# The second layer's modulation, computed beside the first layer's gates and pools instead of beside its dense expert units

## The chip, the cores and the metric

One NeuronCore of a Trainium2 chip; the kernel uses one core. The metric is the device time of one execution in microseconds (us). The engines are named as the profile names them: PE (TensorE, matmuls) and PEld (its weight loads), DVE (VectorE), ACT (ScalarE), POOL (GpSimd) and SP (SyncE, which here issues DMAs only).

## The reference

Two blocks run one after the other on 256 tokens of width 1024, in fp32; the change is within the first. It has two layers, each of a mixer (differential attention, a pool branch and a convolution branch, merged by three sigmoid gates) and of a product-key expert layer. Each layer begins with its modulation:

```python
for l in range(DEPTH):
    mod = (jax.nn.silu(c) @ w_mod[l] + b_mod[l]).reshape(b, N_MOD, 1, d)
    mod_c = (jax.nn.silu(c_ctx) @ w_mod[l] + b_mod[l]).reshape(N_MOD, 1, 1, d)
    ...
    xn = modulate(rms_norm(h, norm1_g[l]), mod[:, 0], mod[:, 1])
    ...
    h = h + mod[:, 2] * mix
    xn2 = modulate(rms_norm(h, norm2_g[l]), mod[:, 3], mod[:, 4])
    h = h + mod[:, 5] * peer_ffn(xn2, ...)
```

`c` and `c_ctx` are inputs, so the modulation of both layers depends on nothing that the layers compute. `w_mod[l]` is 1024 x 6144 in fp32, 25.2 MB a layer.

## The kernel before, in words

**A modulation step.** `modulation(l, pairs)` (line 610) computes two of the six vectors of layer l for each member of `pairs`. For one pair it goes through eight steps, one for each 128 rows of `w_mod`: it loads 1 MB (128 partitions of 2048 numbers) into a raw tile and makes four matmuls with 32 columns of stationary operand each, one in each quarter of the output's partitions (line 626; the trace holds two records for each, eight a step). It yields after each step. After the eighth, the sum is copied by ScalarE (`modsb`), turned by four small matmuls (`ps_modt`, line 634), and VectorE adds the bias into `self.mod`.

A step's raw tile comes from one of three places: a list given to it (the first layer's pair 0, at the kernel's start), a pool given to it (tile `mraw`, lines 619 to 621), or `self.raw` (line 623), which the weight loads use too. In the mixer `self.raw` hands out the two `wraw` tiles by turns. In the first layer's dense expert stage it hands out three by turns: every third comes from the pool of the V units (`vraw`).

**Weights.** `wload` (line 348) loads 1 MB into such a raw tile, and ScalarE and VectorE split it into two units, each of a high part (`uhi`, `vhi`, line 361) and a low part (`ulo`, `vlo`, line 362). There are four units of the `u` kind. A raw tile is free again once both units are split, and a unit can be split once the matmuls on the one that had its place are done. All raw loads are issued by SyncE, whose queue is worked through in order; so are the other engines' queues. The order of each queue is laid down when the program is built, near the order in which the code issues, with instructions moved ahead of others that the builder expects to be ready later.

**The mixer's gate and pool stage.** The first layer works on 512 columns (256 tokens and 256 of context). Its work is paired by hand: `spread` (line 953) runs attention steps, and after each of them as many steps of a second generator, `feed`, as a rate allows (0.75 a step here). In the last part of the attention that second generator is `gate_pool`: eight pieces of weights, 16 products of 24 matmuls of 512 columns each (a pool or a gate), and the pool arithmetic on VectorE and POOL. `weaver` (line 173) puts modulation steps between the products. Of `n` steps it takes one, and then products until their number reaches the share (i + 1) * MODS / n, with MODS = 17. Modulation steps count nothing in the rate, so they come on top. Before, the steps are the 16 of pairs 1 and 2 of the first layer, all through the one tile `mraw`. What is left of the generator when attention ends is run in `mixer_out` (line 1020), ahead of the output product.

**The dense expert stage.** `peer` (line 1092) multiplies through all 16384 experts of the layer in 64 units of 256. In the first layer 384 of the 512 columns go this way, and the other 128 are handled by gathering single rows of u and v (class `Rows`; POOL issues a gather of 128 rows at a time, and VectorE multiplies the rows of u, while TensorE sums those of v in `ps_row`). 42 of the 64 units had their hidden values computed earlier, during routing, and stored in DRAM; the other 22 compute them here. The units go in turns of two and two until the 22 are used up (44 units), and then 20 with stored values follow. One unit loads a V piece (1 MB), the gates G (768 KB), and either a U piece (1 MB) or the stored values (384 KB). Its matmuls: 36 on V (`keep` and `ps_v`, line 1269) and, where hidden values are computed, 48 more (`ps_mm`). For two of the six 512-column products of a unit VectorE adds the result to `racc` (line 1236). The gathers are paced by the TensorE work done, not by time (`Rows.spend`). Before, one modulation step of the second layer is taken at each second unit from the third on (units 2, 4, ... 48), 24 steps in all, with raw tiles of the ring of three.

Of the kernel before, what the change touches and what calls it, by code (L numbers as in the profile page):

```python
# [37 lines left out]
MODS = 17  # L38
# [134 lines left out]
def weaver(main, n, fill, m):  # L173

    done = 0.0
    fill = iter(fill)
    for i, _ in enumerate(islice(main, n)):
        yield 0
        while done * n < (i + 1) * m:
            size = next(fill, None)  # L180
            if size is None:
                break
            done += size
            yield size
    yield from fill
# [144 lines left out]
class Prog:  # L330
# [279 lines left out]
    def modulation(self, l, pairs, raws=None, pool=None, bufs=3):  # L610

        nc, g = self.nc, self.g
        for m2 in pairs:
            ps = self.pm.tile([P, 512], F32, tag="mm", name="ps_mod")
            for k in range(KD):
                src = g["wmod"][l, m2 * KD + k]
                if raws:
                    raw = raws.pop(0)
                elif pool:
                    raw = pool.tile([P, 2048], F32, tag="mraw", name="mraw", bufs=bufs)  # L620
                    nc.sync.dma_start(raw, src)
                else:
                    raw = self.raw("wraw_m")
                    nc.sync.dma_start(raw, src)
                for c in range(4):
                    nc.tensor.matmul(ps[32 * c:32 * c + 32, :], self.sc[:, k, :], raw[:, c * 512:(c + 1) * 512],
                                     start=(k == 0), stop=(k == KD - 1), tile_position=(0, 32 * c))
                if k < KD - 1:
                    yield 0.18
            sb = self.sp.tile([P, 512], F32, tag="t2k", name="modsb")  # L630
            nc.scalar.activation(sb, ps, AF.Copy)
            pp = self.pm.tile([P, 4, 2, 2, 2], F32, tag="mm", name="ps_modt")
            for j in range(4):
                nc.tensor.matmul(pp[:, j].rearrange("p m i s -> p (m i s)"), sb[:, j * P:(j + 1) * P],
                                 self.sel.rearrange("p c s -> p (c s)"), start=True, stop=True)
            for m in (2 * m2, 2 * m2 + 1):
                mod = self.mod[:, l, m]
                b = self.col["bmod", l][:, m * 8:(m + 1) * 8]
                nc.vector.tensor_tensor(mod.rearrange("p (i j) s -> p i j s", i=2), pp[:, :, m % 2].rearrange("p j i s -> p i j s"),
                                        b.rearrange("p (i j) -> p i j", i=2)[:, :, :, None].to_broadcast([P, 2, 4, 2]), op=ALU.add)  # L640
                if m in (1, 4):
                    gn = self.col["n1" if m == 1 else "n2", l]
                    nc.vector.tensor_scalar(mod, mod, 1.0, None, op0=ALU.add)
                    nc.vector.tensor_tensor(mod, mod, gn[:, :, None].to_broadcast([P, KD, 2]), op=ALU.mult)
            yield 0.3
# [261 lines left out]
    def mixer(self, l, xh, xl, T, late, hT):  # L907
        nc, g, tc = self.nc, self.g, self.tc
        qts = list(range(T // P))
        merged = self.mp.tile([P, KD, T], F32, tag="merged", name="merged")  # L910
        self.merged, self.begun, self.pooled = merged, set(), set()
        outer = self.mp
        qkvs, self.done, self.scored, self.whole = {}, set(), set(), set()
        with ExitStack() as right:
            with ExitStack() as cx:
                E = cx.enter_context
                self.mp = E(tc.tile_pool(name=f"att{l}", bufs=1, reuse_waits="tile"))
                self.pa = E(tc.tile_pool(name=f"pa{l}", bufs=2, space=PSUM, reuse_waits="tile"))
                self.pt = E(tc.tile_pool(name=f"pt{l}", bufs=2, space=PSUM, reuse_waits="tile"))
                self.po = E(tc.tile_pool(name=f"po{l}", bufs=1, space=PSUM, reuse_waits="tile"))  # L920
                with tc.tile_pool(name=f"conv{l}", bufs=1, side="right", reuse_waits="tile") as mp:
                    yh = mp.tile([P, KD, T], F32R, tag="yh", name="yh")
                    yl = mp.tile([P, KD, T], F32R, tag="yl", name="yl")
                    conv = self.conv(l, xh, xl, yh, yl, mp, T)
                    next(conv)
                    if late:
                        late()
                    self.ropes(l, self.mp)
                    bulk = Bulk(chain(conv, self.conv_out(l, xh, xl, yh, yl, T)))
                    for _ in self.qkv(l, 0, xh, xl, T, qkvs, islice(bulk, MIX[l][0])):  # L930
                        pass
                    att = Bulk(self.attention(l, qkvs, qts, xh, xl, T))
                    feed = self.feed(l, xh, xl, T, qkvs, bulk)
                    self.steps = 0
                    self.spread(att, feed, MIX[l][2], bulk)
                mp = right.enter_context(tc.tile_pool(name=f"pool{l}", bufs=1, side="right", reuse_waits="tile"))
                mods = self.modulation(0, [1, 2], pool=mp, bufs=1) if l == 0 else iter(())
                bulk.steps, bulk.over = weaver(mods, 16, self.gate_pool(l, xh, xl, mp, T), MODS), False
                self.spread(att, feed, MIX[l][3], att)
            self.mp = outer  # L940
            return self.mixer_out(l, merged, hT, T, right, bulk)
# [150 lines left out]
    def peer(self, l, hT, T, xh, xl):  # L1092
        nc, g, tc = self.nc, self.g, self.tc
        T0, T = T, T - (NROW if l == 0 else 0)
# [5 lines left out]
        with ExitStack() as cx:  # L1100
# [23 lines left out]
            with ExitStack() as c:  # L1124
# [18 lines left out]
                late = []  # L1143
                self.gcur = None
                cur = self.prep(l, jobs[0], xh, xl, T, gd, hd)
                mods = self.modulation(1, range(3)) if l == 0 else iter(())
                for n in range(64):
                    if n % 2 == 0 and n > 1:
                        next(mods, None)
                    nxt = self.prep(l, jobs[n + 1], xh, xl, T, gd, hd) if n < 63 else None  # L1150
                    cur += (self.wload(g[f"v{l}"][jobs[n]], "v"),)
                    if n >= 64 - NLAST and onto:
                        late.append(cur)
                    elif n < 63 or onto:
                        self.values(l, cur, hT, T, keep, rest_acc, n == 0, not onto and n == 62)
                    if n < 1 and onto:
                        self.store_gates(GPARTS)
                    if n < 63:
                        cur = nxt
# [12 lines left out]
                else:  # L1172
                    self.preload("wb0", (1, 3))
                    row = self.rowof(lambda c_: self.mod[:, l, 5, c_, 0:1])
                    xh, xl = (self.xp.tile([P, KD, 512], F32R, tag=nm, name=nm) for nm in ("xh", "xl"))
# [753 lines left out]
```

## Time and profile before

| | |
|---|---|
| time, median of 3 runs | 3701.9 us (3687.57 to 3704.51) |
| the profiled execution's own time | 3701.45 us |
| its span, first to last instruction | 3699.7 us |
| mean granted TensorE clock | 0.985 of full speed |
| TensorE busy | 3574.0 us, 97% of the span |
| VectorE, ScalarE, POOL busy | 67%, 44%, 16% |
| DMA | 777.60 MB, mean 210 GB/s |
| modulation loads in the gate stage | 16 of 1 MB (`mraw`) |
| modulation loads in the dense stage | 24 of 1 MB (`wraw_m`) |

The page divides the span into 40 slices of 92.5 us and gives each engine's busy share in tenths. A window gives for one stretch the busy time of each engine with its number of records, the granted clock, the mean busy share of the 16 DMA engines and what they moved. A wait names the engine and line that waited, what ended the wait, the sum in us, how often, and the longest. In a timeline each row is an instruction with its start and duration, and in brackets the idle time of its engine before it and what ended that. Matmuls are pipelined and their ends are modelled, so records overlap, and a busy TensorE isn't one at its peak.

The first layer's mixer ends at about 700 us of the span, with the gate and pool stage from 490 to 642. Routing follows, and the dense expert stage from 1229 to 2105.

### The profile page before, as it was taken

To read this page: it belongs to the slowest core of one execution; us is meant where nothing else is said; L and a number is where in the kernel's file an instruction comes from. 1 tells how busy PE (TensorE), PEld (TensorE's weight loads), DVE (VectorE), ACT (ScalarE), POOL (GpSimd) and SP (SyncE) were. 2 spreads that over 40 slices of the span, in tenths; PEclk is the share of its full clock that TensorE was granted. 3 is DMA by queue.
4 is the path that set the end of the run, shared out by engine and by line. 5 is a ranking of instruction groups with operands and counts; after the bars stand their busy time and mean duration, and the time that the engine had idled before them with its cause. 6 is when DMAs were issued, how large, how long until landed. Compare 5 with 4: busy or idle time off the path is not lost.

```text
span 3699.7 us, 55016 instructions
## 1 busy us (share of the span) xinstructions
PE 3574.0 (97%) x21681; PEld 3097.0 (84%) x21681; DVE 2461.5 (67%) x4540; ACT 1634.3 (44%) x2608; POOL 604.0 (16%) x686
## 2 busy tenths in 40 slices
PE   7999999899999998999999999999999999999999
PEld 5988877789999877776766799999998888887787
DVE  5566556599697777744445677778876555557675
ACT  3334333336576322222222354555676444445454
POOL 0112222100011232322222121221000000002121
PEclk9999999999999999999999999999999999999999
DMA  5222145224689898888889533354578766766453
GB/s 212 75 86 80 69 154 216 75 83 170 228 323 336 315 332 306 325 295 309 298 321 325 188 115 120 120 175 160 200 269 292 244 236 237 242 231 212 145 174 111
DMA packets 227763, 777.60 MB, mean 210 GB/s; under 512 B 17296, under 2 KB 100752, under 8 KB 168496
## 3 DMA queue, kind: packets, MB, share of 16 engines
q1 hardware_dynamic: 165984, 567.29, 43.7%
q0 software_dynamic: 37184, 135.41, 10.4%
q10 hardware_dynamic: 24336, 71.38, 5.0%
q8 instruction: 170, 2.79, 0.3%
q14 instruction: 89, 0.73, 0.1%
HBM read 705.60 MB, written 68.42 MB: 209 GB/s over the span
## 4 chain that ended last, share of the span: by engine, by line
PE 41%; DVE 4%; DMA 2%; ACT 1%; issue 1%; POOL 1%; DVEq 0%; ACTq 0%; SPq 0%; POOLq 0%
PE keep L1269 12%; PE ps_mm L393 5%; PE ps_mm L395 5%; PE ps_mm L394 5%; PE ps_wide L395 2%; PE ps_wide L393 2%; PE ps_wide L394 2%; PE ps_v L1269 1%; DVE ulo L362 1%; PE ps_nar L393 1%; PE ps_nar L395 1%; PE ps_nar L394 1%; DMA wraw<-in_v 1%; PE ps_mm L414 1%; PE ps_row L307 1%
## 5 line engine op out<-in xcount | busy, mean ns | idle before, releaser
L361 ACT ACTIVATE uhi<-wraw 128x1024 fp32r<-128x1024 f32 x586 | 609.0, 1057 | 879.2 <-PE ps_mm L394 336.1
L393 PE MATMUL ps_mm<-xh,uhi 128*128 128x256 f32 (+2 forms) x2952 | 955.5, 324 | 9.2 <-ACT hs L1566 3.7
L395 PE MATMUL ps_mm<-xh,ulo 128*128 128x256 f32 (+2 forms) x2952 | 940.8, 319 | 7.1 <-DVE ulo L362 7.1
L362 DVE TENSOR_TENSOR ulo<-wraw,uhi 128x1024 fp32r<-128x1024 f32 x586 | 718.0, 1237 | 340.6 <-ACT uhi L361 317.6
L394 PE MATMUL ps_mm<-xl,uhi 128*128 128x256 f32 (+2 forms) x2952 | 939.9, 318 | 0.0
L393 PEld LDWEIGHTS ps_mm<-xh,uhi 128*128 128x128 f32 x2952 | 562.5, 191 | 54.0 <-issue 9.2
L395 PEld LDWEIGHTS ps_mm<-xh,ulo 128*128 128x128 f32 x2952 | 562.2, 191 | 29.4 <-DVE ulo L362 8.0
L394 PEld LDWEIGHTS ps_mm<-xl,uhi 128*128 128x128 f32 x2952 | 562.7, 191 | 20.8
L362 DVE TENSOR_TENSOR vlo<-wraw,vhi 128x1024 fp32r<-128x1024 f32 x184 | 224.0, 1222 | 187.7 <-ACT vhi L361 187.5
L361 ACT ACTIVATE vhi<-wraw 128x1024 fp32r<-128x1024 f32 x184 | 193.2, 1056 | 338.1 <-DMA wraw<-in_v 176.0
L1269 PE MATMUL keep<-vlo,Wh 128*128 128x512 f32 x656 | 256.7, 391 | 3.6 <-DVE vlo L362 3.6
L1269 PE MATMUL keep<-vhi,Wh 128*128 128x512 f32 x656 | 257.8, 393 | 0.5 <-ACT Wh L422 0.5
L1269 PE MATMUL keep<-vhi,Wl 128*128 128x512 f32 x656 | 256.2, 391 | 0.3 <-DVE Wl L423 0.3
L258 POOL DMA_INDIRECT row<-in_urow,eu x128 | 158.5, 1238 | 589.7 <-PE ps_mm L395 440.7
L1213 DVE TENSOR_TENSOR hs_r<-hs_r,G 128x768 f32<-128x768 f32 (+1 forms) x128 | 105.2, 823 | 170.7 <-DMA hs_r<-hd 106.9
L393 PE MATMUL ps_nar<-uhi,xh 128*128 128x256 f32 x704 | 201.3, 286 | 2.3 <-ACT cs L664 2.3
L394 PE MATMUL ps_nar<-ulo,xh 128*128 128x256 f32 x704 | 200.1, 284 | 0.0
L395 PE MATMUL ps_nar<-uhi,xl 128*128 128x256 f32 x704 | 199.9, 284 | 0.0
L258 POOL DMA_INDIRECT row<-in_vrow,ev x128 | 136.0, 1063 | 375.4 <-PE keep L1269 180.2
L1530 ACT ACTIVATE stage<-ps_g 128x512 f32<-128x512 f32 x160 | 165.1, 1160 | 1.7 <-DMA wraw<-in_u 0.8
L274 DVE CUSTOM_DVE_ANT_0 row<-row,xt 128x1024 f32<-128x1024 f32 x128 | 155.2, 1219 | 4.5 <-DMA row<-in_urow,eu 4.5
L1269 PEld LDWEIGHTS keep<-vhi,Wh 128*128 128x128 f32 x656 | 123.7, 189 | 36.8 <-issue 9.2
(428 smaller groups left out, 6965.2 us busy)
## 6 DMA issues: line engine op xcount, KB each, us to landing
wraw<-in_u SPq DMA_DIRECT2D x128, 1024.0 KB
wraw<-in_v SPq DMA_DIRECT2D x128, 1024.0 KB
wraw<-in_wa SPq DMA_DIRECT2D x104, 1024.0 KB
wraw<-in_wb SPq DMA_DIRECT2D x50, 1024.0 KB
gd<-stage ACTq DMA_DIRECT2D x80, 512.0 KB
wraw_m<-in_wmod SPq DMA_DIRECT2D x24, 1024.0 KB
G<-gd SPq DMA_DIRECT2D x31, 768.0 KB
mraw<-in_wmod SPq DMA_DIRECT2D x16, 1024.0 KB
```

The lines of the kernel that those rows point to most:

```text
L258: ins = self.nc.gpsimd.indirect_dma_start(row, None, self.p.g[name], bass.IndirectOffsetOnAxis(ap=idx, axis=0))
L274: ins = nc.vector.tensor_tensor_reduce(out=row, in0=row, in1=self.xt, op0=ALU.mult, op1=ALU.add, scale=1.0, scalar=0.0, accum_out=self.hid ...
L307: nc.tensor.matmul(ps[c:c + 32, :], m[:, g, :], rows[n - 4 + g][:, h * 512:(h + 1) * 512], start=(i == 0), stop=(i == 31), tile_position=( ...
L361: nc.scalar.activation(hi, r, AF.Copy)
L362: nc.vector.tensor_tensor(lo, r, hi.bitcast(F32), op=ALU.subtract)
L393: nc.tensor.matmul(ps, lh, rh, start=(i == 0), stop=False)
L394: nc.tensor.matmul(ps, lh, rl, start=False, stop=False)
L395: self.beat = nc.tensor.matmul(ps, ll, rh, start=False, stop=(i == n - 1))
L414: self.nc.tensor.matmul(ps[:, t0:t1], a[:, s], b[:, k, t0:t1], start=(n == 0 and i == 0), stop=(n == KD - 1 and i == 2))
L1213: nc.vector.tensor_tensor(w, w, G.rearrange("p q j t -> p j q t"), op=ALU.mult)
L1269: self.beat = self.nc.tensor.matmul(ps, a[:, j, t], b[:, c], start=(start and j == 0 and i == 0), stop=(stop and j == 1 and i == 2), skip_ ...
L1530: nc.scalar.activation(st[:, :, tb:tb + 4].rearrange("p j t -> p t j"), pg, AF.Copy, scale=1.0 / GSCALE)
```

## The change

The 24 steps of the second layer's modulation are chained behind the 16 of the first in the weaver of the gate and pool stage, which now spreads 40 steps over its 16 products. The tile `mraw` stays single, and each odd step takes its raw tile from `self.raw` instead, that is, one of the two `wraw` tiles. The dense stage's loop takes no modulation steps any more. By the weaver's sums a product now comes after two or three steps where it came after each step, and the last four steps come after the last product.

```diff
                 if raws:
                     raw = raws.pop(0)
-                elif pool:
+                elif pool and (bufs > 1 or k % 2 == 0):
                     raw = pool.tile([P, 2048], F32, tag="mraw", name="mraw", bufs=bufs)
                     nc.sync.dma_start(raw, src)
                 else:
...
-                mods = self.modulation(0, [1, 2], pool=mp, bufs=1) if l == 0 else iter(())
-                bulk.steps, bulk.over = weaver(mods, 16, self.gate_pool(l, xh, xl, mp, T), MODS), False
+
+                mods = chain(self.modulation(0, [1, 2], pool=mp, bufs=1), self.modulation(1, range(3), pool=mp, bufs=1)) if l == 0 else iter(())
+                bulk.steps, bulk.over = weaver(mods, 40, self.gate_pool(l, xh, xl, mp, T), MODS), False
                 self.spread(att, feed, MIX[l][3], att)
...
                 cur = self.prep(l, jobs[0], xh, xl, T, gd, hd)
-                mods = self.modulation(1, range(3)) if l == 0 else iter(())
                 for n in range(64):
-                    if n % 2 == 0 and n > 1:
-                        next(mods, None)
                     nxt = self.prep(l, jobs[n + 1], xh, xl, T, gd, hd) if n < 63 else None
```

## Rows read from the trace of the kernel before

**Rows 1.** The page's slices (92.5 us): busy tenths, TensorE and DMA engines.

```profile
PE   7999999899999998999999999999999999999999
DMA  5222145224689898888889533354578766766453
```

**Rows 2.** Windows: us; busy us (records) of each engine, PEclk, DMA share, GB/s.

```profile
core 0: us, PE busy (x) PEld busy (x) DVE busy (x) ACT busy (x) POOL busy (x), PEclk, DMA share, GB/s
490.00:642.00 152.00, 151.55 (x774) 112.89 (x773) 88.41 (x156) 55.19 (x121) 34.91 (x55) 1.00 0.54 195
1229.00:1600.00 371.00, 343.60 (x1617) 286.46 (x1617) 270.20 (x371) 107.62 (x130) 119.41 (x96) 0.96 0.87 313
1600.00:1900.00 300.00, 296.84 (x1517) 210.94 (x1516) 133.45 (x183) 79.23 (x94) 82.81 (x79) 1.00 0.87 307
1900.00:1955.00 55.00, 48.98 (x227) 31.67 (x226) 26.74 (x37) 14.18 (x16) 13.21 (x12) 0.95 0.92 347
1955.00:2045.00 90.00, 90.00 (x416) 62.02 (x416) 48.93 (x68) 22.15 (x25) 25.52 (x24) 0.98 0.90 315
```

**Rows 3.** Dense stage in windows of 20 us, columns of rows 2.

```profile
1320.00:1340.00 20.00, 16.09 (x73) 13.33 (x67) 15.57 (x20) 5.02 (x6) 4.39 (x5) 0.91 0.93 362
1340.00:1360.00 20.00, 20.00 (x106) 17.30 (x105) 13.85 (x20) 5.81 (x8) 6.78 (x6) 1.00 0.83 296
...
1380.00:1400.00 20.00, 14.63 (x65) 12.55 (x65) 13.23 (x20) 4.53 (x6) 4.63 (x5) 0.90 0.77 283
```

**Rows 4.** Waits to 1600 us (us, times, longest), TensorE and ScalarE.

```profile
PE ps_mm L393 <- DVE racc L1236: 16.1, 6, 4.5
...
ACT uhi L361 <- DMA wraw<-in_v: 97.1, 12, 14.2
```

**Rows 5.** Timeline of VectorE at one hole (start us, us, instruction, idle).

```profile
1329.22 2.36 DVE L362 TENSOR_TENSOR ulo<-wraw,uhi 128x1024 fp32r<-128x1024 f32 x2 [2.71 <-ACT uhi L361]
...
1332.64 0.68 DVE L1236 TENSOR_TENSOR racc<-racc,ps_v 128x512 f32<-128x512 f32 x1
```

**Rows 6.** SyncE's waits, 1600 to 1955 us.

```profile
SPq L351 <- PE ps_mod L626: 42.4, 9, 9.7
```

**Rows 7.** Timeline of TensorE, one modulation step, dense stage.

```profile
1319.52 0.40 PE L1269 MATMUL ps_v<-uhi,Wl 128*128 128x512 f32 x1
1319.85 1.06 PE L626 MATMUL ps_mod<-wraw_m,sc 128*32 128x512 f32 x8
1320.84 0.50 PE L1269 MATMUL keep<-uhi,Wh 128*128 128x512 f32 x1
1321.18 0.39 PE L1269 MATMUL keep<-ulo,Wh 128*128 128x512 f32 x1
```

**Rows 8.** Window of the kernel's start, columns of rows 2.

```profile
15.00:20.00 5.00, 3.98 (x11) 2.30 (x12) 1.03 (x3) 0.00 (x0) 1.03 (x1) 1.00 1.01 421
```

**Rows 9.** Timelines of SyncE, then ScalarE, in the gate stage.

```profile
529.89 0.33 SPq L621 DMA_DIRECT2D mraw<-in_wmod  x1
530.27 0.42 SPq L975 DMA_DIRECT2D pwr<-in_wa  x1
...
560.55 8.14 SPq L621 DMA_DIRECT2D mraw<-in_wmod  x2
...
570.22 0.43 SPq L975 DMA_DIRECT2D pwr<-in_wa  x1
...
535.36 0.63 ACT L422 ACTIVATE pwh<-pwr 128x512 fp32r<-128x512 f32 x1 [6.84 <-DMA pwr<-in_wa]
...
577.58 0.63 ACT L422 ACTIVATE pwh<-pwr 128x512 fp32r<-128x512 f32 x1 [6.71 <-DMA pwr<-in_wa]
```

**Rows 10.** Gate stage: ps_mod's window, idle before mraw's matmuls, SyncE's wait.

```profile
490.00:642.00 152.00, 17.05 (x128) 2.52 (x128) 1.04 (x2) 1.00 0.54 195
...
  issue: 2.7, 11
...
SPq L621 <- PE ps_mod L626: 59.6, 15, 9.1
```

## The prediction

> **What bounds the kernel now.** I began with the page's slices [rows 1]: TensorE is at 9 tenths nearly throughout, so the question is what its busy time hides in the two stages that the change touches. The slices show where they differ: in slices 12 to 22, which hold the dense stage, the DMA engines are at 8 or 9 tenths, in the mixer before it (slices 2 to 8) at 1 to 5. The change carries 24 loads of 1 MB out of the first stretch into the second.
>
> Then the stages by themselves [rows 2]. The gate and pool stage (490 to 642 us) has TensorE busy 151.55 of 152 us at full clock, with 195 GB/s: bound by TensorE, with no hole in it. The dense stage runs from 1229 to 2105 us, and falls into three. To 1600 us, while rows of u are gathered, TensorE is idle for 27.4 of 371 us and its granted clock is 0.96; DMA is at 313 GB/s. From 1600 to 1900 it is idle for 3.2 of 300 us. From 1900 to 1955 it is idle for 6.0 of 55 us at clock 0.95, at 347 GB/s. After 1955, when the last modulation load is done, it is not idle at all (90.00 of 90). The work is of one kind from 1900 us on (units with no hidden products), so its records tell the pace: without the 24 of modulation 203 in 55 us before 1955, 3.7 a us, and 416 in 90 us after it, 4.6 a us.
>
> [...] What ends a hole is mostly the sum into racc on VectorE, 16.1 us in six waits, and that stands in VectorE's queue behind the split of a weight unit that waited, by way of ScalarE, for a V load: 97.1 us of ScalarE's waits are for wraw<-in_v [rows 4]. Around 1329 us VectorE is seen to stand 2.71 us before ulo, and racc comes only after it [rows 5]. So V loads land late. They are late because SyncE issues them late: a raw tile must first be free, and a modulation raw is free only when TensorE has reached its matmuls; SyncE waited 42.4 us for that from 1600 on [rows 6].
>
> [...]
>
> **The change, part by part.**
>
> *Matmuls of a modulation step.* One step is 8 records in 1.06 us (24 steps: three pairs of eight in the code); from its start to the next matmul are 0.99 us, and the matmuls on its two sides stand 0.10 and 0.11 us further apart than the usual 0.23 [rows 7]. That is 1.2 us a step, 24 x 1.2 = 28.8 us that leave the dense stage, where TensorE sets the pace but for the holes. They come into the gate stage, which has 0.45 us idle to take them in: with two or three steps in a row some edges are shared, so 24 x 0.99 = 24 at least, 28.8 at most; I take 26. The three transpositions with their copies and additions move too, as much out of the one stage as into the other: nothing in the sum.
>
> *Loads out of the dense stage.* 25.2 MB leave a stretch of 726 us. What they are worth beyond the matmuls: to 1600 us, the holes (27.4 us) and the slow clock after them. Window by window the clock's loss is 4% of 371 = 15 us, of which some 6 lie within the holes. I take 60% of 27.4 + 9 = 36, that is 22: two of the ring's eight loads in four units are modulation, but the row gathers that stay load VectorE and the DMA queues as before. From 1600 to 1900: 2 of 3.2. From 1900 to 1955: 203 records at the later pace of 4.6 a us are 44 us, so 11 us, of which three steps are 3.6; of the other 7.5 I take 5. With 28.8 the dense stage gives 28.8 + 22 + 2 + 5 = 58 us. Bounds: 28.8 if no wait goes; 28.8 + 36 + 3 + 8 = 76 if all go. SyncE's order, the ring's turn (every third raw comes from the v pool) and the row pacing, which counts TensorE's work and not time, stay as they are but for the missing places.
>
> *Loads into the gate stage.* There, 16 steps went with 16 products, all through the single tile mraw; now 40 do, by turns through mraw and the two wraw tiles, which the weights of the same stage use. The page's 195 GB/s x 152 us = 29.6 MB become 54.8 MB in about 178 us, 308 GB/s; the start of the kernel moves 421 with the same 8 KB rows [rows 8], so bandwidth isn't short. Time from issue to landing is: the last of three loads (a mraw, a wraw, a quarter MB) issued from 568.4 to 570.2 us is awaited until 577.6, 9.2 us; with one mraw ahead, issued at 529.9, the quarter MB is there at 535.4, 5.5 us [rows 9]. Without its steps a product and its share of attention takes (152 - 17.05) / 16 = 8.4 us. Two steps come with 0.8 product: 6.7 + 2.0 = 8.7 us of cover for two loads and 0.4 weight load. It is near even. Where three steps stand in a row and the first uses mraw, the third waits for a load begun after the first: 5.5 - 1 = 4.5 us open. By the weaver's sums that is at steps 12 to 14, 26 to 28 and, with no product left, 36 to 39: 13 us. Before, none was: TensorE lost 2.7 us at all 16 steps [rows 10], with 9.5 us of cover each, though SyncE waited 59.6 us for ps_mod. Bounds: nothing, as the queues' order is laid out anew when the program is built and other products may stand in between; and 20 pairs x (9.2 - 8.7 + 2.4 for the splits) = 57 us if each pair ends on its loads (2.36 us for two on VectorE [rows 5], ScalarE's taken as long). I take 13, nearest to the rows of before, where the queue held.
>
> *Behind the loads.* On SyncE the weights of the last gates, the four loads of old and the first of w_out stand behind the last four steps. TensorE then has the six merged splits to wait for anyhow; within the 13. The first layer's modulation is complete earlier, the second's long before its use behind the dense stage: nothing. POOL's queue has none of these DMAs.
>
> **Sum.** -58 + 26 + 13 = -19 us. The profiled execution is 3701.45 us (span 3699.7 and 1.75 around it), the median of the three runs 3701.9, so the two agree: 3701.9 - 19 = **3683**.
>
> **Rivals.** *A, the gate stage becomes bound by its raw tiles.* Its pairs end on loads, not on TensorE: 26 + 57, against 58: +25, 3727; with only 28.8 from the dense stage +54, 3756. It decides the sign from 32 us of stalls on (58 - 26), 1.6 us a pair. For it: cover and load time are near even, SyncE is in order and already waits 59.6 us for ps_mod. Against: not one product waited before, and split weights lie up to four units ahead. [...]
>
> *B, the dense stage's holes have another cause.* VectorE is busy 270 of 371 us to 1600 [rows 2], much of it with row products that stay; if they are what delays the splits, only 28.8 us come back, and the gate stage takes 26 to 31: 3699 to 3704. For it: holes nearly vanish after 1600 us (3.2 of 300 us) though modulation goes on, when VectorE's busy time falls to 133 of 300. Against: after the last modulation load none is left.
>
> *C, the dense stage was bound by DMA.* 25.2 MB at 313 GB/s are 80 us; TensorE's own work holds that to 76. With 13 + 26 in the gate stage, 3665; with no stalls there, 3652. For it: 347 GB/s where the units take 55 us. Against: from 1600 to 1900 TensorE is full at 307 GB/s.
>
> **How the numbers follow.** A measurement of this kernel can tell about 0.5%, 18.5 us, from no change. The forecast (0.42) lies across that bound, -8 to -32; I put 0.25 of it on faster. C has 0.20, all faster. B has 0.19, all same. A has 0.19, 0.17 of it slower by over 18.5 us. Slower by over that for reasons of the rebuilt order takes 0.04 more from the forecast. So faster 0.45, same 0.34, slower 0.21. The range reaches to C's 3652 and over most of A, to 3724; the likeliest case by itself is 3670 to 3694.
>
> **What would show it.** Right: ps_mod in the gate stage with 320 records, that stage 30 to 50 us longer; from 1229's counterpart on no ps_mod, the 60 us period at 53 to 56 us, clock above 0.97, the dense stage 50 to 65 us shorter. Wrong by A: TensorE idle before ps_mod or before the gates' ps_mm, by a DMA of mraw, wraw_m or wraw, over 32 us in all. Wrong by B: holes of 4 us still there with no modulation near them.

## The result and the profile after

The changed kernel takes 3650.85 us (median of 4 runs, 3646.74 to 3653.45), the kernel before 3699.03 (median of 4, 3687.57 to 3704.51). The ratio is 0.9871 with a 95% interval of 0.9852 to 0.9889: 48 us faster. The forecast was 3683, 19 us faster, in a range from 3652 to 3724. The direction was right, the gain more than twice the forecast, and the time 1.2 us below the range.

Where did it go? I cut both executions at the same events. The first is `old`, the residual that is added behind the mixer's output product; the next is the first `keep` matmul, with which the dense stage begins. The slices answer [rows 1]: what they had at 8 and 9 tenths of DMA in the dense stage is still there, and the mixer's slices 6 to 8 have gone from 4, 5 and 2 tenths to 5, 7 and 6.

Page of the kernel after, busy tenths of TensorE and the DMA engines in slices of 91.2 us:

```profile
PE   7999999989999999999999999999999999999999
DMA  5222257623479999988799433354677766666343
```

The addition of `old` in the trace of the kernel before (first and last start, in us, stand after the durations):

```profile
L1088 DVE SCALAR_TENSOR_TENSOR hT<-ps_mm,mod,old x16: 473/475/484, 660.7 to 697.6; 128x256 f32<-128x256 f32 x16
```

The same in the kernel after, and under it the matmuls of modulation:

```profile
L1089 DVE SCALAR_TENSOR_TENSOR hT<-ps_mm,mod,old x16: 474/477/484, 701.7 to 738.6; 128x256 f32<-128x256 f32 x16
...
L626 PE MATMUL ps_mod<-mraw,sc x160: 592/592/617, 497.1 to 679.9; 128*32 128x512 f32 x160
L626 PE MATMUL ps_mod<-wraw_m,sc x160: 592/592/617, 504.3 to 680.8; 128*32 128x512 f32 x160
```

So all 320 matmuls lie in the gate and pool stage, half of them through `mraw`, half through the two `wraw` tiles, and the mixer ends 41.0 us later (660.7 to 701.7).

The dense stage I divide where the rows of `u` are done and the first rows of v are summed (first `ps_row`). *Part 1* is from the first `keep` to there, *part 2* from there to the last matmul that reads `racc`. Windows of the kernel before, with the columns of rows 2:

```profile
1243.20:1598.20 355.00, 327.60 (x1524) 271.32 (x1522) 258.47 (x355) 101.07 (x122) 112.90 (x90) 0.96 0.86 313
1598.20:2109.60 511.40, 502.21 (x2492) 352.61 (x2492) 245.91 (x348) 136.39 (x160) 132.90 (x127) 0.99 0.84 300
```

Windows of the kernel after, the gate and pool stage first:

```profile
490.00:702.00 212.00, 202.47 (x1073) 138.71 (x1072) 98.58 (x182) 63.23 (x133) 40.80 (x55) 0.98 0.71 267
1283.90:1580.80 296.90, 296.90 (x1420) 258.86 (x1418) 257.57 (x351) 100.82 (x121) 112.98 (x90) 1.00 0.94 334
1580.80:2060.70 479.90, 479.90 (x2382) 347.58 (x2381) 243.83 (x342) 135.49 (x158) 141.86 (x127) 1.00 0.84 292
```

| us | before | after | difference |
|---|---|---|---|
| start to the first `old` | 660.7 | 701.7 | +41.0 |
| first `old` to the first `keep` (routing) | 582.5 | 582.2 | -0.3 |
| dense, part 1 | 355.0 | 296.9 | -58.1 |
| dense, part 2 | 511.4 | 479.9 | -31.5 |
| last `racc` to the end | 1590.1 | 1589.2 | -0.9 |
| span | 3699.7 | 3649.9 | -49.8 |

In the dense stage TensorE now has no idle time at all, and the granted clock is 1.00. The 58.1 us of part 1 are three things. 27.4 us are idle time that is gone (355.0 - 327.60). 14.4 are, by the estimate of 1.2 us a step, the matmuls of 12 steps. The other 16.3 of the busy time (327.60 - 296.90 - 14.4) are for the most part work that TensorE did slowly behind holes: by estimate, a granted clock of 0.96 over 355 us is a loss of some 14 us. Another 1.0 us is busy time of the four matmuls that turn a finished pair (`ps_modt`), and the rest is open. The groups show the slow work: the matmuls that follow most holes took 398 ns each on average and take 338 now.

Lines of part 1, kernel before (busy us, mean ns, then idle us before them and what ended it):

```profile
L393 PE MATMUL ps_mm<-xh,vhi 128*128 128x384 f32 x96 | 38.2, 398 | 23.4 <-DVE racc L1236 16.1 <-ACT uhi L361 7.3
```

At the hole of [rows 5] the clock falls behind the hole and not in it. Windows of the hole and of the 5 us after it, kernel before (the last three numbers are the clock, the DMA share and GB/s):

```profile
1329.00:1334.00 5.00, 1.09 (x6) 0.66 (x5) 4.78 (x6) 1.13 (x2) 1.51 (x1) 1.00 1.01 412
1334.00:1339.00 5.00, 5.00 (x22) 5.00 (x21) 3.28 (x5) 2.00 (x2) 0.00 (x0) 0.66 0.86 354
```

From 1334.7 to 1338.0 us the clock was 0.51, and the `ps_mm` matmuls of 384 columns began 0.32 us apart there, against 0.18 just before and after. It was not so behind every hole: in windows from each of the six on (1274.0 to 1282.0, 1333.4 to 1341.4, 1388.8 to 1405.5, 1450.7 to 1462.8, 1512.0 to 1524.0 and 1571.0 to 1586.7 us) the clock was 0.62, 0.79, 0.80, 0.58, 0.86 and 1.00, and in the rest of part 1 it was 0.99 or 1.00.

The group of matmuls in the kernel after:

```profile
L393 PE MATMUL ps_mm<-xh,vhi 128*128 128x384 f32 x96 | 32.5, 338 | 0.0
```

In part 2 the 31.5 us are 14.4 of matmuls, 9.2 of idle time (511.40 - 502.21) and 7.9 of other busy time: a granted clock of 0.99 over 511 us is, by the same estimate, a loss of some 5 us, and `ps_modt` was busy for 2.9. In part 1 ScalarE's 97.1 us of waits for `wraw<-in_v` [rows 4] are gone; it now stands waiting for TensorE to be done with a unit, so the loads are ahead.

Waits in part 1 of the kernel after, ScalarE:

```profile
ACT uhi L361 <- PE ps_v L1267: 88.3, 18, 5.7
```

In part 1 the DMA engines moved 313 GB/s before and move 334 now without a hole. So it wasn't their rate that bound the stage. What else about the 24 steps cost 61 us beyond their own matmuls (89.6 - 28.8) was the question for the experiments.

### The profile page after: what moved, and what is told of

Same layout as the page of the kernel before. It is cut to its first block, busy times and chain, and to the rows that moved or that the text cites. A ratio compares the mean times of both kernels' runs of the same rounds, so it can differ in the third digit from the quotient of the medians.

```text
span 3649.9 us, 55044 instructions
## 1 busy us (share of the span) xinstructions
PE 3550.4 (97%) x21681; PEld 3087.9 (85%) x21681; DVE 2459.1 (67%) x4540; ACT 1636.0 (45%) x2608; POOL 613.7 (17%) x686
## 4 chain that ended last, share of the span: by engine, by line
PE 86%; DVE 6%; DMA 3%; ACT 2%; POOL 2%; issue 1%; ACTq 0%; SPq 0%; DVEq 0%; POOLq 0%
PE keep L1267 19%; PE ps_mm L393 13%; PE ps_mm L395 13%; PE ps_mm L394 13%; PE ps_v L1267 5%; PE ps_nar L393 2%; PE ps_nar L395 2%; PE ps_nar L394 2%; PE ps_mm L414 2%; PE ps_wide L395 2%; PE ps_wide L393 2%; PE ps_wide L394 2%; PE ps_row L307 2%; DVE ulo L362 1%; PE ps_mod L626 1%
## 5 line engine op out<-in xcount | busy, mean ns | idle before, releaser
L258 POOL DMA_INDIRECT row<-in_vrow,ev x128 | 144.6, 1129 | 328.8 <-PE keep L1267 160.6
```

Source lines behind the costliest of these rows:

```text
L258: ins = self.nc.gpsimd.indirect_dma_start(row, None, self.p.g[name], bass.IndirectOffsetOnAxis(ap=idx, axis=0))
```

## The experiments

Three things go with a step besides its matmuls: its bytes (25.2 MB in all), its turn among the ring's raw tiles with SyncE's wait for it, and, as came out later, a PSUM tile (`ps_mm`, `ps_v` and `ps_mod`, which the matmuls write their sums to, are such tiles). The medians and the ratios below are of all runs, the ratios to the kernel before on the same chip. First `old`, the parts and the span come from one profiled execution of each kernel, cut as above. The four kernels that share the dense stage of the kernel after (after, 8, 10, 11) took 776.3 to 776.8 us in it.

| kernel | first `old` | part 1 | part 2 | dense | span | median us | ratio to before (95%) |
|---|---|---|---|---|---|---|---|
| before | 660.7 | 355.0 | 511.4 | 866.4 | 3699.7 | 3699.0 | |
| after | 701.7 | 296.9 | 479.9 | 776.8 | 3649.9 | 3650.9 | 0.9871 (0.9852 to 0.9889) |
| 1 own tiles | 660.2 | 325.6 | 500.9 | 826.5 | 3660.1 | 3658.2 | 0.9896 (0.9841 to 0.9951) |
| 2 ring, thin loads | 660.9 | 357.4 | 501.9 | 859.3 | 3691.2 | 3680.9 | 0.9961 (0.9949 to 0.9974) |
| 3 loads only | 702.1 | 296.8 | 482.1 | 778.9 | 3667.9 | 3675.9 | 0.9951 (0.9934 to 0.9968) |
| 4 gate stage, thin loads | 692.9 | 297.0 | 480.6 | 777.6 | 3639.1 | 3640.4 | 0.9848 (0.9799 to 0.9898) |
| 5 own tiles, POOL's queue | 660.6 | 325.5 | 499.5 | 825.0 | 3661.0 | 3663.2 | 0.9902 (0.9882 to 0.9923) |
| 6 ring, late | 661.6 | 297.6 | 532.7 | 830.3 | 3660.3 | 3661.2 | 0.9895 (0.9875 to 0.9915) |
| 7 own tiles, late | 661.3 | 296.9 | 520.4 | 817.3 | 3646.0 | 3649.5 | 0.9874 (0.9857 to 0.9892) |
| 8 the changed kernel again | 704.5 | 296.8 | 480.0 | 776.8 | 3650.2 | 3652.0 | 0.9876 (0.9859 to 0.9893) |
| 9 own tiles, thin loads | 660.8 | 323.3 | 496.8 | 820.1 | 3655.4 | 3653.6 | 0.9883 (0.9858 to 0.9908) |
| 10 all through `mraw` | 804.8 | 296.9 | 479.7 | 776.6 | 3749.9 | 3755.0 | 1.0163 (1.0143 to 1.0184) |
| 11 MODS = 16 | 708.1 | 296.8 | 479.5 | 776.3 | 3656.7 | 3657.2 | 0.9891 (0.9873 to 0.9909) |
| 12 split 8 + 16 | 678.2 | 296.9 | 498.9 | 795.8 | 3641.0 | 3650.0 | 0.9877 (0.9858 to 0.9895) |
| 13 PSUM tile held | 701.1 | 319.8 | 480.7 | 800.5 | 3671.8 | 3672.5 | 0.9921 (0.9892 to 0.995) |

**1. Own tiles.** The kernel before, its dense stage's steps with tiles of their own, four of 512 columns each from the pool of work tiles. The bytes and matmuls stay; the turn in the ring goes.

```diff
-                    raw = self.raw("wraw_m")
-                    nc.sync.dma_start(raw, src)
+                    raw = None
...
+                    if raw is None:
+                        mv = self.sp.tile([P, 512], F32, tag="t2k", name="mq")
+                        nc.sync.dma_start(mv, src[:, c * 512:(c + 1) * 512])
+                    else:
+                        mv = raw[:, c * 512:(c + 1) * 512]
```

> The kernel before, with the 24 steps in the dense stage as they were, but each step's 1 MB comes as four loads of 256 KB into work tiles of 2 KB a partition, and not into the ring of three raw tiles. Bytes and matmuls stay, the place in the ring is gone. Theory ring (a modulation raw holds a place until TensorE reaches it, so V and U loads are issued late): the holes go, and the dense stage, from the first keep to the last of racc, takes what it takes after the change plus the matmuls, 777 + 29 = 806 us; time about 3640. Theory bytes (25 MB too many for the DMA engines): the holes stay, 845 to 866 us; time 3680 to 3700.

**2. Ring, thin loads.** The kernel before; the steps keep their turn in the ring, but load 64 columns of 2048 and multiply these again and again. This kernel, like the others with thin loads, leaves the second layer's modulation out.

```diff
-                    nc.sync.dma_start(raw, src)
+                    nc.sync.dma_start(raw[:, :64], src[:, :64])
...
-                    nc.tensor.matmul(ps[32 * c:32 * c + 32, :], self.sc[:, k, :], raw[:, c * 512:(c + 1) * 512],
+                    mv = raw[:, c * 512:(c + 1) * 512] if raws is not None or pool else raw[:, None, :64].to_broadcast([P, 8, 64])
+                    nc.tensor.matmul(ps[32 * c:32 * c + 32, :], self.sc[:, k, :], mv,
```

> The kernel before, with the same 24 ring places and matmuls, but each load brings 64 of 2048 columns (32 KB in place of 1 MB), and the matmuls read these 64 again and again: the second layer's modulation is not computed. Theory ring: the holes stay, dense stage 850 to 866 us, time 3685 to 3700. Theory bytes: they go, 806 us, time about 3640. If each has a part, it lies between, and with e1 the two shares add up.

Without the bytes the dense stage is only 7.1 us shorter, and none of it in part 1. Without the turn it is 39.9 us shorter, with all the bytes still there, at 343 GB/s. The profiled execution of experiment 2 was the slowest of its eight (3692.96 us; they begin at 3671.77), so its 7.1 us may be too few; what the medians say stands behind the fourth corner. Window of part 1 in experiment 1, with the columns of rows 2:

```profile
1245.10:1570.70 325.60, 316.42 (x1523) 261.68 (x1521) 258.44 (x355) 101.31 (x122) 108.27 (x90) 0.99 0.95 343
```

And in experiment 2:

```profile
1244.20:1601.60 357.40, 327.09 (x1523) 269.78 (x1521) 258.30 (x355) 101.17 (x122) 111.53 (x90) 0.96 0.80 279
```

Experiment 2 has the holes of before with a tenth fewer bytes a second (279 against 313): the turn makes them. ScalarE waits for V loads there as long as before [rows 4]; in experiment 1 its list has no wait for a load. In experiment 2:

```profile
ACT uhi L361 <- DMA wraw<-in_v: 103.2, 13, 13.1
```

But 9.2 us of idle time stayed in experiment 1 (325.60 - 316.42), most of it for the same releaser, `racc`, and its dense stage took 826.5 us where 806 were expected; so the turn is not all.

Waits of TensorE in part 1, experiment 2:

```profile
PE ps_mm L393 <- DVE racc L1237: 20.2, 6, 6.2
```

The same in experiment 1:

```profile
PE ps_mm L393 <- DVE racc L1240: 8.1, 5, 3.6
```

**9. Own tiles, thin loads**, the fourth corner: experiment 1 with 64 columns of each 512 loaded.

```diff
-                        nc.sync.dma_start(mv, src[:, c * 512:(c + 1) * 512])
+                        nc.sync.dma_start(mv[:, :64], src[:, c * 512:c * 512 + 64])
+                        mv = mv[:, None, :64].to_broadcast([P, 8, 64])
```

> e1 (work tiles, old places in the dense stage) with 64 of 512 columns a load, read again and again (the second layer's modulation is not computed): no ring place and an eighth of the bytes; the fourth corner beside before, e1 and e2. The u row part took 355.0 us before, 325.6 in e1, 357.4 in e2, 296.9 after. If the 14 us by which e1 stands over 296.9 and 12 matmul steps (14.4) are bytes, this one takes 310 to 314 us there; if they come from the matmuls' and work tiles' order, 322 to 327. The whole: 3645 against 3658.

What each corner's dense stage takes beyond the 776.8 us of the kernel after:

| | in the ring | own tiles | worth of the turn |
|---|---|---|---|
| all bytes | 89.6 (58.1 and 31.5) | 49.7 (28.7 and 21.0) | 39.9 |
| thin loads | 82.5 (60.5 and 22.0) | 43.3 (26.4 and 16.9) | 39.2 |
| worth of the bytes | 7.1 | 6.4 | |

In these executions the two add up nearly without regard to each other. By the ratios of the whole time (0.9961, 0.9896 and 0.9883 for experiments 2, 1 and 9), the ring's bytes are worth some 14 us, those of own tiles 5, and the turn 38 and 29. So the turn is the larger by either account, but its size is less sure than the table looks. Own tiles differ from the ring in two more ways, four loads in place of one and a place given back after one matmul in place of four, which were not taken apart.

With neither turn nor bytes 43.3 us remain, of which 28.8 are matmuls. 14.5 us were open, 12.0 of them in part 1 (26.4 - 14.4). TensorE's longest wait in part 1 of experiment 9 is still this:

```profile
PE ps_mm L393 <- DVE racc L1241: 6.7, 5, 3.6
```

**5. Own tiles, POOL's queue.** Perhaps the loads stand in SyncE's queue ahead of weights while they wait for a work tile. Experiment 1 with POOL issuing them:

```diff
-                        nc.sync.dma_start(mv, src[:, c * 512:(c + 1) * 512])
+                        nc.gpsimd.dma_start(mv, src[:, c * 512:(c + 1) * 512])
```

> e1 with the 256 KB loads issued by POOL in place of SyncE; nothing else. e1 left 21 us in the dense stage over 777 + 29. If they are SyncE standing before a modulation load until TensorE frees a work tile (32.9 us of such waits to 1575 us), the dense stage comes to 806 to 812 us and the time to about 3640; if they are bytes, it stays at 822 to 830 and the time at 3655 to 3660. A third way: POOL's row gathers stand behind the loads and the stage gets longer than in e1.

The wait in question, SyncE in part 1 of experiment 1:

```profile
SPq L627 <- PE ps_mod L630: 32.9, 8, 7.0
```

825.0 us against 826.5: who issues them made no difference, and SyncE's order behind these loads isn't the 14.5.

**13. PSUM tile held.** The sums of a step's pair stay in `ps_mod` over eight steps, that is some 15 units, and `ps_mod` is one of the three tiles of the pool in which `ps_mm` and `ps_v` take turns. To test this by itself, the kernel after holds such a tile in its dense stage as long as a pair would, from one small matmul to another, with no modulation:

```diff
+                    if l == 0 and n in (2, 18, 34):
+                        held = self.pm.tile([P, 512], F32, tag="mm", name="ps_mod")
+                        ins = nc.tensor.matmul(held[0:32, 0:P], self.sc[:, 0, :], self.ident, start=True, stop=False, tile_position=(0, 0))
+                        ...
+                    if l == 0 and n in (16, 32, 48):
+                        ins = nc.tensor.matmul(held[0:32, 0:P], self.sc[:, 0, :], self.ident, start=False, stop=True, tile_position=(0, 0))
+                        ...
+                        sb = self.sp.tile([P, 512], F32, tag="t2k", name="modsb")
+                        nc.scalar.activation(sb[0:32, 0:P], held[0:32, 0:P], AF.Copy)
```

> The kernel after; in the dense stage a product's PSUM tile (one of the three that ps_mm and ps_v take turns in) is claimed at units 2, 18 and 34 by one small matmul and given back at units 16, 32 and 48 by a second and a copy. No modulation, no load, no ring place: only the bank is held, as ps_mod held it before the change. e9, with neither ring place nor bytes, still stands 43.3 us over the kernel after in the dense stage, 28.8 of it matmuls with their edges. If the held bank is the other 14.5 us (two tiles in turn for ps_mm and ps_v, so TensorE waits for racc), this one takes 308 to 312 us in the u row part (296.9 after) and about 791 in the dense stage, time about 3666, with waits for racc in TensorE's list. If the 14.5 us are a matter of the modulation's matmuls themselves, 297 and 777, time 3651.

Six small matmuls and a held tile cost 22.9 us in part 1, where 11 to 15 were expected, and 0.8 in part 2. Of the 22.9, 12.0 are idle time and 10.9 longer busy time (307.81 - 296.90), at a granted clock of 0.97. Windows of experiment 13:

```profile
1284.60:1604.40 319.80, 307.81 (x1428) 265.88 (x1426) 258.09 (x351) 100.98 (x122) 109.70 (x90) 0.97 0.88 311
1604.40:2085.10 480.70, 480.70 (x2385) 347.01 (x2385) 245.26 (x342) 136.04 (x160) 140.29 (x127) 1.00 0.83 291
```

Waits of TensorE in its part 1:

```profile
PE ps_mm L393 <- DVE racc L1243: 12.0, 6, 3.4
```

The wait is the one of before [rows 4]. With a third tile free, in the kernel after, TensorE has no wait for `racc` in part 1; with the third held, it waits 12.0 us in six places for VectorE, late with its queue, to add a `ps_v` to `racc`. VectorE is busy 258 of 320 us in part 1 and 245 of 481 in part 2; I take that for the reason why it is late only in the first, but no run changes its load alone. 22.9 us is more than the 12.0 that experiment 9 left open there: the two costs are not simply added, and I take it that steps of modulation fill part of such waits with their own matmuls. That last was not tested.

**6 and 7. Late steps.** If VectorE's load in part 1 makes the holes, steps that begin at unit 25 should leave few or none. Experiment 6 is the kernel before, experiment 7 is experiment 1, with this edit each:

```diff
-                    if n % 2 == 0 and n > 1:
+                    if n >= 24 and n % 5 < 3:
                         next(mods, None)
```

> The kernel before, its 24 steps through the ring as before, but at units 25 to 62, three in five, when the rows of v are gathered, and none in the first 24 units. Theory ring: the first 24 units take 297 to 302 us with no hole, as after the change, and the holes move to where the steps are, smaller there, since 12 steps in that part cost 32 us in all before (14.4 of it matmuls): 24 steps 64 us. Dense stage 835 to 845 us, time about 3672. If the holes belong to the u row part and not to the steps, that part still takes about 340 us.

> e1's work tiles at e6's units: no ring place, and in the part where the DMA engines have room (292 GB/s after the change). Theory ring: only matmuls and their edges are left, dense stage 806 to 812 us; the mixer is as before the change (41 us shorter than after it), so the time is 3638 to 3645, faster than both kernels. If bytes count there too, 815 us or more and no faster than the kernel after.

Part 1 falls to 297.6 and 296.9, that of the kernel after, and part 2 takes it on: 52.8 and 40.5 us more than after, for 24 steps whose matmuls are 28.8. So the holes of part 1 go with its steps, and the turn in the ring costs part 2 something also (24.0 against 11.7 beyond the matmuls). In both, the longest wait of TensorE in part 2 is at the matmuls that turn a finished pair, experiment 6 first:

```profile
PE ps_modt L634 <- DVE mask L300: 6.3, 1, 6.3
PE ps_modt L638 <- DVE mask L300: 5.0, 1, 5.0
```

Windows of part 2, experiment 6:

```profile
1537.70:2070.40 532.70, 519.42 (x2598) 357.19 (x2597) 246.27 (x352) 138.37 (x161) 130.70 (x127) 0.98 0.87 310
```

Experiment 7:

```profile
1536.80:2057.20 520.40, 513.82 (x2596) 355.15 (x2596) 245.10 (x352) 137.15 (x161) 136.76 (x127) 0.99 0.88 314
```

I had hoped experiment 7 would beat the changed kernel, with 806 to 812 us in the dense stage. It took 817.3 there, and at 3649.5 it equals the changed kernel (3650.9 and 3652.0).

**3. Loads only.** The kernel after, with the 24 loads put back into the dense stage into work tiles that nobody multiplies:

```diff
+                    if l == 0 and n % 2 == 0 and 2 <= n <= 48:
+                        for c in range(4):
+                            mq = self.sp.tile([P, 512], F32, tag="t2k", name="mq")
+                            nc.sync.dma_start(mq, g["wmod"][1, n // 2 - 1][:, c * 512:(c + 1) * 512])
+                            nc.vector.tensor_copy(mq[:, 0:2], mq[:, 2:4])
```

> The kernel after, with 24 MB loaded in the dense stage at the old places, in loads of 256 KB into work tiles, and no matmul on them (VectorE copies 2 columns of each): bytes alone come back. Theory ring: dense stage 777 to 785 us, time 3651 to 3660. Theory bytes: 820 us or more, the holes are back, time 3695 or more.

It tells nothing of the dense stage. As nothing paced the loads there, the built order put most of them into routing. Tile `mq` of experiment 3, in the window from 800 to 1300 us:

```profile
L1151 SPq DMA_DIRECT2D mq<-in_wmod x76: 327/422/1205, 854.8 to 1037.1; - x76
```

76 of 96 were issued there, and what got longer is routing (first `old` to first `keep` 598.7 us, against 582.2). The question that it was made for is answered by the four corners instead.

**4. Gate stage, thin loads.** The kernel after, the second layer's steps loading 64 columns of 2048. What is left of the 41 us in the mixer is then not the loads':

```diff
-                    nc.sync.dma_start(raw, src)
+                    nc.sync.dma_start(raw[:, :64] if l else raw, src[:, :64] if l else src)
...
+                    mv = raw[:, None, :64].to_broadcast([P, 8, 64]) if l else raw[:, c * 512:(c + 1) * 512]
```

> The kernel after, with the second layer's 24 steps in the gate stage, but loading 64 of 2048 columns each and reading these again and again (the second layer's modulation is not computed). Tiles, order and matmuls stay. If loads cost 13 us in the gate stage, as in the prediction, the mixer shortens by about 13 us, time 3638; if the 41 us by which the mixer grew are matmuls and their edges and the raw tiles' turns, it stays within 4 us of 3651.

Its first `old`:

```profile
L1090 DVE SCALAR_TENSOR_TENSOR hT<-ps_mm,mod,old x16: 473/476/485, 692.9 to 729.7; 128x256 f32<-128x256 f32 x16
```

That is 8.8 us earlier than in the kernel after (11.6 earlier than in its second run), at 161 GB/s instead of 267, and TensorE is idle for 2.6 us of the stage instead of 9.5. Window of experiment 4:

```profile
490.00:693.00 203.00, 200.38 (x1077) 138.81 (x1077) 97.96 (x182) 62.62 (x133) 40.17 (x57) 0.98 0.44 161
```

So the bytes of the loads cost about 9 of the 41 us, or somewhat more; the matmuls, with their edges and turns, are the other 32.

**10. All through `mraw`.** The change's first hunk undone, so that all 40 steps use the single tile:

```diff
-                elif pool and (bufs > 1 or k % 2 == 0):
+                elif pool:
```

> The kernel after with one part of the change undone: all 40 steps of the gate stage go through the single tile mraw, none through wraw. If load time is what matters there, each second step of a row of two or three waits for a load of 4.9 us begun after the step before, some 3 us open at 20 or more places: mixer 40 to 70 us longer than after the change, time 3690 to 3720. If the built order puts products in between, at most 10 us, 3660.

3755 us, 1.6% slower than the kernel before. Window of its gate stage:

```profile
490.00:805.00 315.00, 232.84 (x1076) 147.70 (x1075) 97.33 (x182) 62.84 (x133) 37.73 (x57) 0.80 0.50 181
```

Waits of TensorE between 480 and 840 us in experiment 10:

```profile
PE ps_mod L626 <- DMA mraw<-in_wmod: 65.4, 19, 4.9
```

TensorE is idle for 82.2 of the 315 us (315.00 - 232.84), and its clock is 0.80, where the gate stage of the kernel after has 0.98. In the kernel after the same wait is nearly nothing; TensorE from 480 to 740 us:

```profile
PE ps_mm L395 <- DVE ulo L362: 5.3, 2, 2.6
PE ps_mod L626 <- DMA mraw<-in_wmod: 1.9, 1, 1.9
```

**11. MODS = 16.** The constant that I read as leaving four steps together at the end, set to 16:

```diff
-MODS = 17
+MODS = 16
```

> The kernel after with MODS 16 in place of 17: the same 40 steps, the last product after step 38 in place of 36, so two steps, not four, stand behind it. If the 1.9 us at a load of mraw and the idle around 656 to 684 us come from that row of four, the mixer shortens by 2 to 6 us, time 3646 to 3650; else no difference, 3652.

The first `old` comes 6.4 us later than in the kernel after (3.6 later than in its second run), and the time is 6 us longer: nothing is to be won there.

**12. Split 8 + 16.** Both places in part: pair 0 of the second layer in the gate stage, pairs 1 and 2 late in the dense stage with work tiles. In the gate stage the steps go by turns through `mraw` and `wraw`, as in the change.

```diff
+                mods = chain(self.modulation(0, [1, 2], pool=mp, bufs=1), self.modulation(1, [0], pool=mp, bufs=1)) if l == 0 else iter(())
+                bulk.steps, bulk.over = weaver(mods, 24, self.gate_pool(l, xh, xl, mp, T), MODS), False
...
+                mods = self.modulation(1, [1, 2]) if l == 0 else iter(())
                 for n in range(64):
-                    if n % 2 == 0 and n > 1:
+                    if n >= 24 and n % 5 < 2:
```

> Of the second layer's 24 steps 8 go to the gate stage (24 there, by turns through mraw and wraw) and 16 to the dense stage's units 24 to 61 through work tiles of 256 KB loads. 8 in the gate stage at 1.2 us and little waiting: 10 to 13 us; 16 in the v row part at e7's 40.5 / 24 = 1.7 us: 27; together 37 to 40 against 41 after the change and 40.5 in e7: 3645 to 3650, no more than 0.2% under the kernel after. If waits grow faster than the number of steps in either place, it is less: 3638 to 3644.

Its part 2 has no hole; the window:

```profile
1553.50:2052.40 498.90, 498.90 (x2525) 351.10 (x2525) 244.49 (x348) 136.51 (x160) 136.51 (x127) 1.00 0.88 310
```

16 steps cost it 19.0 us over the kernel after (19.2 are their matmuls), and the mixer is 23.5 us shorter than there. The profiled execution took 3641.0, but the timed runs lie from 3642.8 to 3654.1 with a median of 3650.0: no gain that these measurements can tell.

**8. The changed kernel again**, beside the last ones on their chip:

> The kernel after as it is, on the same chip as e7, for the comparison: 3647 to 3654.

## Why the prediction was right in sign and wrong in size

**What fails** is *Loads out of the dense stage*: with the matmuls 58 us, with a bound of 76, and measured 89.6. Four things were wrong in it, three in its size and one in its cause.

- *The share of holes.* 60% was taken, since two of eight loads were modulation and the gathers stayed. All went: idle time gave 36.6 us where 16.4 + 2 + 5 = 23.4 were taken. A turn in the ring is not worth its share of the loads. By itself it is worth 39.9 us of the dense stage, with all its consequences, by experiments 1 and 2 (29 to 38 by the whole times). Why it costs so much is not shown. That SyncE stands before a modulation load, with everything behind it, is not enough: in part 1 of experiment 1 it stood 32.9 us so, and no V load came late.
- *The slow clock.* Of the 15 us of clock loss to 1600 us, 6 were put within the holes and left out, and 60% of the rest taken, 5.4. No run shows the 6: windows that hold the longest idle stretch of each hole have the clock at 0.85 to 1.00, some 1 us of loss together. At the hole of 1329 us the idle time and the slow work after it are separate (clock 1.00, then 0.66), and all of the slow work went: by estimate from the granted clock some 14 us in part 1 and 5 in part 2. 19 against 5.4 is nearly 14 us, beside 13 of idle time, of the miss of 32. The bound of 76 had only 9 us for this term.
- *The turning of finished pairs.* It was put at nothing, as it moves from the one stage into the other. Out of the dense stage alone it took 3.9 us of busy time (1.0 and 2.9), and some 1 us of the miss stays open.
- *The PSUM tile.* The reasoning knew raw tiles alone. Experiment 13 has the wait for `racc` of rows 4 from a held PSUM tile alone (12.0 us, where the kernel after has none), so part of that wait was there because `ps_mod` held one of three; how large a part is not shown. The gain was booked under the right holes, but with one cause short.

**What held.** *Matmuls of a modulation step*, 28.8 us: 16 steps in experiment 12 cost 19.0, with the turning of two pairs, where 19.2 were expected from rows 7. *The gate stage*, 26 + 13 = 39: measured 41.0. That the sum is so near is luck, as its parts missed in opposite ways: experiment 4 has 9 for the loads and 32 for the rest. The 13 us were to be waits of a third step for `mraw`; the list of waits has 1.9, and the larger one is 5.3 for the split weights. *Behind the loads*, nothing: routing has -0.3 us, and all that follows the dense stage -0.9.

Two kinds of tile were at work, a raw tile of the ring (39.9 us of the dense stage by experiments 1 and 2) and one of PSUM (23.7 by experiment 13), and all 27.4 us went. With all of the 36 us taken in place of 22, the forecast would have been 14 us lower, 3669, and still 18 us too high.

**The rivals.** *B* falls: no hole is left after the change. Its observation was good, though: I take VectorE's load (258 of 320 us, and 245 of 481) for the reason why two PSUM tiles cost 22.9 us in part 1 and 0.8 in part 2 of experiment 13, which no run tests by itself. *C* named times nearest to the result, 3665 and 3652, for a reason that is not so: bytes are worth 7 us by the stages, some 14 by the whole times, where C had 76, and 334 GB/s go without a hole. That was luck. *A* was a real mechanism that the change holds off by its first hunk. In experiment 10, without that hunk, the mixer ends 103 us later and the kernel is slower than before; with it, at 1.9 us of such waits, the point of 32 us was never near. For experiment 10 I had expected less, 40 to 70 us, and it cost more, as the clock fell with it (0.80 against 0.98): busy time in the stage is 30.4 us longer (232.84 against 202.47). TensorE's waits for the single tile are 65.4 us there; in the changed kernel the turns of `wraw` are the second buffer.

Of what should show it right, the 320 records and the longer gate stage came as said (41 in 30 to 50), the clock too (1.00, above 0.97). The dense stage is 89.6 us shorter where 50 to 65 were named, and the period of 60 us (the holes of rows 3 lie in windows that begin 60 us apart), that of four units in part 1, is 49.5 us (296.9 / 6) where 53 to 56 were.

## What to carry to other kernels

Side work that borrows from a ring of buffers costs here by the place it holds more than by its bytes: price what waits for that place, and look for every pool from which it holds a tile, PSUM included. When idle time of TensorE is to go, add the slow work after the holes as a term of its own; here it was, by estimate from the granted clock, some 19 us beside 37 of idle time. And before side work is moved to a stage with bandwidth to spare, give it a second tile there: that decided between 48 us faster and 56 slower.

## What the runs showed of the hardware

- The slow work after a hole: in part 1 of the kernel before, with six holes in 355 us and 27.4 us of idle time, the granted clock was 0.96, by estimate a loss of some 14 us beside the idle time; after the change, without a hole, it was 1.00. The groups show 398 ns against 338 for the same matmul. Around one hole the clock was 1.00 in the 5 us that hold it and 0.66 in the next 5; behind five of the six it was 0.58 to 0.86, behind the sixth 1.00.
- The DMA engines moved 334 GB/s over 297 us with TensorE never waiting, and 343 GB/s over 326 us, at a busy share of 0.94 and 0.95. A busy share of 0.86 with holes looked like a limit and wasn't one.
- One PSUM tile out of three, held and doing nothing, costs 7.7% of part 1 (22.9 of 296.9 us) and 0.2% of part 2. VectorE is busy 81% of the one and 51% of the other; that this is the reason is my reading, which no run tests by itself.
